# Two changes of written order in a decoder layer: sums ahead of low parts in gate and up, and one step of putting together per pair in down

## The chip, the cores and the metric

The kernel runs on one core of one Trainium2 chip. The number that counts is the device time of one execution in microseconds (us). The kernel before was timed three times: 2296.75 us is the median, 2289.06 the lowest and 2296.81 the highest. A further execution was recorded by the profiler; every duration below comes from it.

The engines of the core are named as in the profile: PE (TensorE, matrix products; PEld is its loading of weights), DVE (VectorE, elementwise on two inputs), ACT (ScalarE, elementwise on one input), POOL (GpSimd, here an issuer of transfers and a little elementwise work) and SP (SyncE, here the issuer of most transfers). Each engine takes its own instructions strictly in its own order; between engines there are only semaphores.

## The reference

One layer of a decoder on 512 tokens of width 2048, in fp32: an RMS norm, attention with two groups of heads, an output projection and a residual add; then a second RMS norm and a SwiGLU block with 5632 hidden columns, and a residual add. The change touches the last part alone:

```
def _swiglu(h, w_gate, w_up, w_down):
    return (jax.nn.silu(h @ w_gate) * (h @ w_up)) @ w_down
...
        h = _rms_norm(x, ffn_norm[l])
        x = x + _swiglu(h, w_gate[l], w_up[l], w_down[l])
```

## The kernel before

**Numbers in two parts.** PE multiplies in a rounded fp32 type. To keep fp32 accuracy each operand is split: ACT copies it into the rounded type, which gives the high part (`act(..., AF.Copy)`), and DVE subtracts that copy from the operand, which gives the low part (`tt(..., op=OP.subtract)`). Three products (high by high, high by low, low by high) then stand for one.

**Seven products in place of eight.** Gate, up and down use a scheme in which a product of 2 by 2 blocks takes seven block products of sums and differences of blocks in place of eight. The sums of the weight blocks are made on the chip; the results are put together again afterwards.

**Gate and up** (the loop from line 866 on) work on 176 groups of weights: 22 pairs of hidden column blocks `j`, gate and up of each (`which`), and four groups `g` along the contraction. Group `i` has these steps:

- `fetch(i)` (line 701): SP loads a 512 KB tile `r` of four weight blocks. There are three such buffers, so `fetch(i + 4)` can be issued only when everything that reads group `i + 1`'s tile is done. The last of these is the low part.
- `sums(i)` (line 713): three DVE additions that write four more blocks into the same tile.
- `parts(i)` (line 728, by `part_steps`): ACT writes the high part of seven blocks (1792 columns), DVE the low part. They go into one of two halves of `bigm`, so group `i` writes where group `i - 2` was. The copy on ACT also paces one transfer from the POOL queue per group (`sum_weights`, line 112), which adds up weight blocks of down in device memory for later.
- 42 matmuls (line 901): 28 with the high part of the weights, then 14 with the low part.
- `next(pending)` (line 920): one step of the work behind an earlier column block. `evict` reads the finished sums from PSUM, `gate_out` multiplies by the norm's factor and applies SiLU, `up_out` multiplies gate by up, forms block sums and stores them as `ad` for down. Four steps after a gate block and four after an up block fill the eight groups of a pair `j`.

The order of all this on each engine is the order in which the program writes it, because `pin` (line 67) tells the scheduler to keep it from the last output projection on. Matmuls are placed by the scheduler. In group `i` the kernel before writes: `parts(i + 1)`, `fetch(i + 4)`, `sums(i + 2)` (lines 877 to 881), the matmuls, `next(pending)`.

**Down** runs four passes over 22 pairs of hidden blocks (`ps_` = 0 to 3; two halves of the output, each with a first pass of four products and a second of three). For each pair `splits` (line 836) makes high and low parts of a down weight tile and of an activation tile, and PE runs 48 matmuls in the first passes, 36 in the second. PSUM holds the sums of one pass. `keep1` saves those of a first pass in `ca` and `cb`; `finish_late` (line 956) puts the results of the first half of the output together, block by block (`q` = 0 to 3), in steps that are taken during the third pass (`ps_` = 2). Two steps are taken per pair of that pass, one in the others (lines 1022 and 1023). A step is a DVE addition, subtraction or product; two of them also need the residual, which POOL loads into the single buffer `acc` from `x1d`, and POOL stores the result to `out`. `fold` and `fold_early` do the same for the second half of the output in the last pass, and `finish` ends the kernel.

Of the kernel before, what the change touches and what calls it, by code (L numbers as in the profile page):

```python
# [62 lines left out]
def hybrid_layer(ctx: ExitStack, tc: tile.TileContext, xT, vec, ffb, wfg, wfirst, win, cmpw, wout, wgu, wdn, out):  # L63
# [772 lines left out]
    def splits(i):  # L836
        second, j = pass_of(i)[1:]
        n = 3 if second else 4
        m, at = WAT[i % 4]
        w = [cut(m, at + h * 4 * T, n * T) for h in range(2)]  # L840
        m, at = AAT[i % 3]
        a = [cut(m, at + h * 4 * 256, n * 256) for h in range(2)]
        split2(a, rawa.pop(i))
        if second:
            r, t = raww.pop(i), t2(j)
            tt(r[:, T:2 * T], r[:, :T], t, op=OP.add)
            split2([x[:, 2 * T:] for x in w], t)
            split2([x[:, :2 * T] for x in w], r[:, :2 * T])
        else:
            split2(w, raww[i])  # L850
        return [[x.rearrange("p (f c) -> p f c", f=n) for x in y] for y in (w, a)]

    SETS = (("s", "s", "t", "o"), ("g", "g", "m", "t"))
# [16 lines left out]
    for j in range(NJ):  # L870
        for which in range(2):
            q = [ps.tile([P, T], F32, tag=tag, name=f"q{which}{j}_{i}", bufs=BUFS[tag])
                 for i, tag in enumerate(SETS[which])]
            for g in range(NG):
                i = (2 * j + which) * NG + g

                if 3 <= i < LAST:
                    parts(i + 1)
                    fetch(i + 4)
                if 2 <= i < LAST - 1:  # L880
                    sums(i + 2)
                if i == 4:
                    split(fr2, acc)
                if i == LAST - 2:
                    live["fa"] = ffp.tile([P, 2 * FORM + OFF_FORM], F32, tag="fa", name="rawm", bufs=1)
                    for n in range(2):
                        load_a(n)
                        run(load_w(n))
                elif i >= LAST - 1:
                    ahead[i - LAST + 1] = splits(i - LAST + 1)  # L890
                w = split_w.pop(i)

                for wp in range(2):
                    for kk in range(2):
                        k = 2 * (ORDER[i] % NG) + kk
                        a = forms[k]
                        cs = slice(kk * P, (kk + 1) * P)
                        for fa, fb, b, h in PROD:
                            o = q[b][:, h * 256:(h + 1) * 256]
                            for xp in range(2 - wp):  # L900
                                nc.tensor.matmul(o, w[:, wp, fb, cs], a[:, xp, fa],  # L901
                                                 start=(k == 0 and h == 0 and wp == 0 and xp == 0),
                                                 stop=(g == NG - 1 and kk == 1 and wp == 1), skip_group_check=True)
# [33 lines left out]
    def fold(y, s4, s62=None):  # L937

        tt(halves(y[1]), halves(y[1]), both(s4), op=OP.subtract)
        yield  # L940
        tt(y[0][:, :256], y[0][:, :256], y[1][:, :256], op=OP.subtract)
        yield
        if s62 is not None:
            tt(y[0], y[0], s62, op=OP.add)
            yield

    def fold_early(q):

        y = [k[:, q] for k in kept]
        yield from fold(y, y[0][:, 256:])  # L950
# [5 lines left out]
    def finish_late(q, b):  # L956
# [3 lines left out]
        act(s4, b[1][:, :256], AF.Copy)  # L960
        yield
        y = [k[:, q] for k in kept]
        tt(s4, s4, y[0][:, 256:], op=OP.add)
        yield from fold(y, s4, s62)
        for i in range(2):
            pin(nc.gpsimd.dma_start(acc, x1d[2 * q + i]))
            tt(y[i], y[i], rstd, op=OP.mult)
            yield
            tt(y[i], y[i], acc, op=OP.add)
            pin(nc.gpsimd.dma_start(out[2 * q + i], y[i]))  # L970
            yield

    def finish(q, b):

# [12 lines left out]
    for ps_ in range(4):  # L987
# [16 lines left out]
        def block(js, parts, end=None):  # L1004
# [124 lines left out]
```

## Time and profile before

| | us |
|---|---|
| median of three runs (lowest, highest) | 2296.75 (2289.06, 2296.81) |
| the profiled execution | 2287.78 |
| its span, first to last instruction | 2286.0 |
| PE busy | 2187.9 |
| DVE busy | 1703.7 |
| ACT busy | 1007.0 |

In the span, the groups of gate and up run from 875 us to 1842 us, down from there to the end. Times in a row of the profile count from the span's start. In the view of groups of instructions, a row gives the line, the engine, the operation, the tile that is written and those read, shapes and count; then the busy time in us and the mean of one instruction in ns; then the engine's idle time just before these instructions, and who ended it. Line 71 is `tt` and line 74 `act`, the helpers that record every such operation, so that the tile's name tells which one it is: `bigm<-r,bigm` on DVE is a low part, `bigm<-r` on ACT a high part, `r<-r` on DVE the sums, and `q` the matmuls of gate and up; `pd` are those of down. Matmuls overlap in PE's pipeline: a row that says 280 ns for one of them does not mean that each takes 280 ns of PE's time.

### The profile page before, as it was taken

The page shows a single profiled execution, that of the slowest core. Times are in us where ns is not written, and L with a number is a line of the kernel's source. Part 1 is how long each engine was busy: PE and PEld are TensorE (multiplying, and loading weights), DVE is VectorE, ACT ScalarE, POOL GpSimd, SP SyncE. Part 2 cuts the span into 40 slices and gives each one's busy share as a digit, 9 for nine tenths or more (in the row PEclk, how much of TensorE's full clock was granted, in tenths as well). Part 3 has the DMA queues.
Part 4 walks back from the last instruction along what each step waited for, and adds up shares of the span by engine and source line. Part 5 has one row for each costly group of instructions (what it writes and reads, how often), then busy time and mean ns, then how long its engine had stood idle before and what let it go on. Part 6 is the DMA issues. An engine that isn't in the chain of part 4 may idle for free.

```text
span 2286.0 us, 37104 instructions
## 1 busy us (share of the span) xinstructions
PE 2187.9 (96%) x15207; PEld 1984.8 (87%) x15207; DVE 1703.7 (75%) x2488; ACT 1007.0 (44%) x1231; POOL 172.6 (8%) x283
## 2 busy tenths in 40 slices
PE   8999999999999999999999999999999999999898
PEld 6878878788787889888888888898888899999898
DVE  5677577555565547888878888888888897888888
ACT  5555455444454334333333333333333355564453
POOL 0000000000100000111111111111111100000000
PEclk9999999999999999999999999999999999999999
DMA  5421211222223444667766666766666698468854
GB/s 180 148 65 38 74 47 56 75 81 76 77 80 106 142 153 136 160 161 172 163 163 166 165 165 158 177 162 163 172 161 162 164 356 299 147 230 286 292 155 144
DMA packets 111740, 347.47 MB, mean 152 GB/s; under 512 B 13392, under 2 KB 13392, under 8 KB 111568
## 3 DMA queue, kind: packets, MB, share of 16 engines
q1 hardware_dynamic: 83808, 268.21, 35.5%
q0 software_dynamic: 22144, 52.44, 14.0%
q10 hardware_dynamic: 5616, 24.43, 3.3%
q8 instruction: 119, 1.95, 0.3%
q14 instruction: 53, 0.43, 0.1%
HBM read 316.46 MB, written 74.71 MB: 171 GB/s over the span
## 4 chain that ended last, share of the span: by engine, by line
PE 50%; DVE 28%; ACT 14%; issue 6%; DMA 2%; POOL 0%; ACTq 0%; SPq 0%; DVEq 0%; POOLq 0%
DVE bigm L71 14%; ACT bigm L74 12%; DVE r L71 9%; PE pd L1029 7%; PE q L901 5%; PE pd L1034 4%; PE po L143 2%; PE po L141 2%; PE po L142 2%; DVE cb L71 2%; DMA acc<-x1d 1%; PE ps_qf L141 1%; PE ps_qf L142 1%; PE ps_qf L143 1%; PE ps_vf L141 1%
## 5 line engine op out<-in xcount | busy, mean ns | idle before, releaser
L74 ACT ACTIVATE bigm<-r 128x1792 fp32r<-128x1792 f32 x175 | 298.4, 1705 | 604.7 <-DVE r L71 478.1
L71 DVE TENSOR_TENSOR bigm<-r,bigm 128x1792 fp32r<-128x1792 f32 x175 | 354.3, 2024 | 149.0 <-ACT bigm L74 149.0
L71 DVE TENSOR_TENSOR r<-r 128x512 f32<-128x512 f32 x525 | 268.7, 512 | 14.6 <-DMA r<-wgu 2.5
L901 PE MATMUL q<-formy,bigm 128*128 128x256 f32 x1848 | 223.8, 280 | 20.5 <-ACT bigm L74 20.5
L901 PE MATMUL q<-forma,bigm 128*128 128x256 f32 x1848 | 224.7, 281 | 17.6 <-ACT bigm L74 17.6
L901 PEld LDWEIGHTS q<-formy,bigm 128*128 128x128 f32 x1848 | 215.3, 188 | 28.9 <-ACT bigm L74 28.9
L901 PE MATMUL q<-bigm 128*128 128x256 f32 x1848 | 224.3, 280 | 16.1 <-ACT bigm L74 16.1
L901 PE MATMUL q<-formx,bigm 128*128 128x256 f32 x1848 | 223.8, 280 | 16.2 <-ACT bigm L74 16.2
L901 PEld LDWEIGHTS q<-forma,bigm 128*128 128x128 f32 x1848 | 216.2, 189 | 26.2 <-ACT bigm L74 26.1
L901 PEld LDWEIGHTS q<-bigm 128*128 128x128 f32 x1848 | 215.8, 188 | 24.4 <-ACT bigm L74 24.4
L901 PEld LDWEIGHTS q<-formx,bigm 128*128 128x128 f32 x1848 | 215.2, 188 | 24.5 <-ACT bigm L74 24.5
L116 POOL DMA_DIRECT2D wsum<-wdn x176 | 120.1, 682 | 1016.9 <-ACT bigm L74 901.7
L1029 PE MATMUL pd<-bigm 128*128 128x256 f32 x1224 | 153.0, 280 | 8.8 <-DVE bigm L71 6.2
L1029 PEld LDWEIGHTS pd<-bigm 128*128 128x128 f32 x1224 | 146.6, 191 | 10.2 <-DVE bigm L71 6.8
L71 DVE TENSOR_TENSOR bigm<-wd,bigm 128x2048 fp32r<-128x2048 f32 (+1 forms) x64 | 110.3, 1724 | 26.6 <-ACT bigm L74 26.6
L74 ACT ACTIVATE bigm<-wd 128x2048 fp32r<-128x2048 f32 (+1 forms) x64 | 93.7, 1465 | 72.6 <-DVE wd L71 50.8
L143 PE MATMUL po<-bigm,wp_o 128*128 128x512 f32 x256 | 99.8, 390 | 0.8 <-DVE wp_o L71 0.8
L141 PE MATMUL po<-bigm,wp_o 128*128 128x512 f32 x256 | 99.8, 390 | 0.0
L142 PE MATMUL po<-bigm,wp_o 128*128 128x512 f32 x256 | 99.6, 389 | 0.0
L74 ACT ACTIVATE bigm<-rawm 128x768 fp32r<-128x768 f32 (+2 forms) x72 | 65.7, 921 | 62.4 <-PE pd L1034 57.7
L71 DVE TENSOR_TENSOR bigm<-rawm,bigm 128x768 fp32r<-128x768 f32 (+2 forms) x72 | 75.9, 1054 | 12.1 <-ACT bigm L74 12.0
L1034 PE MATMUL pd<-bigm 128*128 128x256 f32 x612 | 81.3, 277 | 0.0
(478 smaller groups left out, 4092.3 us busy)
## 6 DMA issues: line engine op xcount, KB each, us to landing
r<-wgu SPq DMA_DIRECT2D x175, 512.0 KB, 4.5
wsum<-wdn POOLq DMA_DIRECT2D x176, 256.0 KB, 4.8
rawm<-ad SPq DMA_DIRECT2D x44, 512.0 KB, 6.3
wd<-wdn SPq DMA_DIRECT2D x40, 512.0 KB, 5.8
wd<-wsum SPq DMA_DIRECT2D x40, 512.0 KB, 6.7
ad<-cb ACTq DMA_DIRECT2D x22, 896.0 KB, 4.6
rawm<-ad SPq DMA_DIRECT2D x44, 384.0 KB, 3.7
ws_o<-wout SPq DMA_DIRECT2D x32, 512.0 KB, 3.5
```

The lines of the kernel that those rows point to most:

```text
L71: return pin(nc.vector.tensor_tensor(*args, op=op))
L74: return pin(nc.scalar.activation(*args, **kw))
L116: d = nc.gpsimd.dma_start(step[0], step[1], **step[2])
L141: nc.tensor.matmul(o, lh, rh, start=start, stop=False)
L142: nc.tensor.matmul(o, lh, rl, start=False, stop=False)
L143: nc.tensor.matmul(o, ll, rh, start=False, stop=stop)
L901: nc.tensor.matmul(o, w[:, wp, fb, cs], a[:, xp, fa], start=(k == 0 and h == 0 and wp == 0 and xp == 0), stop=(g == NG - 1 and kk == 1 and ...
L1029: nc.tensor.matmul(b[q][k][:, h * 256:(h + 1) * 256], w[0][:, fb, q * P:(q + 1) * P], a[xp][:, fa], start=(j == 0 and h == 0 and xp == 0), ...
L1034: nc.tensor.matmul(b[q][k][:, h * 256:(h + 1) * 256], w[1][:, fb, q * P:(q + 1) * P], a[0][:, fa], start=False, stop=(j == NJ - 1), skip_g ...
```

## The change

In the loop of gate and up `sums(i + 2)` is written ahead of `parts(i + 1)` and `fetch(i + 4)`. `finish_late` is written anew: five steps per block `q` in place of seven, one step per pair in the third pass in place of two, block 1 ahead of block 0, and each load of the residual is issued two steps ahead of the step that adds it. `fold` goes into `fold_early` without a change to what that does. In the very last of the 88 pairs of down, the activation tile is split after the weight tile.

```
@@ splits
-        split2(a, rawa.pop(i))
+        if i < 4 * NJ - 1:
+            split2(a, rawa.pop(i))
...
         else:
             split2(w, raww[i])
+        if i == 4 * NJ - 1:
+            split2(a, rawa.pop(i))
@@ gate and up, group i
+                if 2 <= i < LAST - 1:
+                    sums(i + 2)
                 if 3 <= i < LAST:
                     parts(i + 1)
                     fetch(i + 4)
-                if 2 <= i < LAST - 1:
-                    sums(i + 2)
@@ finish_late
         y = [k[:, q] for k in kept]
-        tt(s4, s4, y[0][:, 256:], op=OP.add)
-        yield from fold(y, s4, s62)
-        for i in range(2):
+
+        def residual(i):
             pin(nc.gpsimd.dma_start(acc, x1d[2 * q + i]))
-            tt(y[i], y[i], rstd, op=OP.mult)
-            yield
+
+        def put(i):
             tt(y[i], y[i], acc, op=OP.add)
             pin(nc.gpsimd.dma_start(out[2 * q + i], y[i]))
-            yield
+
+        residual(1)
+        tt(s4, s4, y[0][:, 256:], op=OP.add)
+        tt(halves(y[1]), halves(y[1]), both(s4), op=OP.subtract)
+        yield
+        tt(y[0][:, :256], y[0][:, :256], y[1][:, :256], op=OP.subtract)
+        tt(y[0], y[0], s62, op=OP.add)
+        yield
+        tt(y[1], y[1], rstd, op=OP.mult)
+        put(1)
+        residual(0)
+        yield
+        tt(y[0], y[0], rstd, op=OP.mult)
+        yield
+        put(0)
+        yield
@@ block
-            for _ in range(1 + (ps_ == 2)):
-                next(pending, None)
+            next(pending, None)
```

More of the change, by code (lines that the diff above doesn't have):

```diff
@@ L935, in keep1, with fold_early @@
         tt(halves(kept[1][:, q]), halves(b[1]), both(kept[0][:, q, :256]), op=OP.add)
-    def fold(y, s4, s62=None):
-        tt(halves(y[1]), halves(y[1]), both(s4), op=OP.subtract)
+    def fold_early(q):
+        y = [k[:, q] for k in kept]
+        tt(halves(y[1]), halves(y[1]), both(y[0][:, 256:]), op=OP.subtract)
         yield
@@ L942, in fold @@
         yield
-        if s62 is not None:
-            tt(y[0], y[0], s62, op=OP.add)
-            yield
-    def fold_early(q):
-        y = [k[:, q] for k in kept]
-        yield from fold(y, y[0][:, 256:])
         for i in range(2):
@@ L962, in finish_late @@
         y = [k[:, q] for k in kept]
-        tt(s4, s4, y[0][:, 256:], op=OP.add)
-        yield from fold(y, s4, s62)
-        for i in range(2):
+        def residual(i):
             pin(nc.gpsimd.dma_start(acc, x1d[2 * q + i]))
-            tt(y[i], y[i], rstd, op=OP.mult)
-            yield
+        def put(i):
             tt(y[i], y[i], acc, op=OP.add)
             pin(nc.gpsimd.dma_start(out[2 * q + i], y[i]))
-            yield
+        residual(1)
[13 more added lines that the diff above has]
+        yield
     def finish(q, b):
```

## The prediction

> **What bounds the kernel now.** I read the page's engine shares first, then the groups of instructions, the list of waits, the chain that ended last, and then one stretch of gate and up in order of time.
>
> ```profile
> span 2286.0 us, 37104 instructions
> PE 2187.9 (96%) x15207; PEld 1984.8 (87%) x15207; DVE 1703.7 (75%) x2488; ACT 1007.0 (44%) x1231; POOL 172.6 (8%) x283
> L74 ACT ACTIVATE bigm<-r 128x1792 fp32r<-128x1792 f32 x175 | 298.4, 1705 | 604.7 <-DVE r L71 478.1
> L71 DVE TENSOR_TENSOR bigm<-r,bigm 128x1792 fp32r<-128x1792 f32 x175 | 354.3, 2024 | 149.0 <-ACT bigm L74 149.0
> L71 DVE TENSOR_TENSOR r<-r 128x512 f32<-128x512 f32 x525 | 268.7, 512 | 14.6 <-DMA r<-wgu 2.5
> PE q L901 <- ACT bigm L74: 70.4, 169, 2.0
> ```
>
> PE looks full at 96%, but in 169 of 176 groups it waits for a high part, the high parts wait for the sums (478.1 us), and the low parts wait for the high parts (149.0 us). That is a ring of two engines that wait for each other in turn. In order of time (start, duration, engine):
>
> ```profile
> 1304.18 2.02 DVE L71 TENSOR_TENSOR bigm<-r,bigm 128x1792 fp32r<-128x1792 f32 x1 [0.84 <-ACT bigm L74]
> 1304.20 5.05 PE L901 MATMUL q<-formy,bigm 128*128 128x256 f32 x42 [0.67 <-ACT bigm L74]
> 1306.13 1.60 DVE L71 TENSOR_TENSOR r<-r 128x512 f32<-128x512 f32 x3
> 1307.90 1.71 ACT L74 ACTIVATE bigm<-r 128x1792 fp32r<-128x1792 f32 x1 [3.75 <-DVE r L71]
> 1309.64 2.02 DVE L71 TENSOR_TENSOR bigm<-r,bigm 128x1792 fp32r<-128x1792 f32 x1 [0.98 <-ACT bigm L74]
> 1309.66 5.04 PE L901 MATMUL q<-bigm 128*128 128x256 f32 x42 [0.41 <-ACT bigm L74]
> ```
>
> Low part of one group, sums of the next, its high part, its low part: 1304.18 to 1306.13 (1.95), to 1307.90 (1.77), to 1309.64 (1.74), together 5.46 us. This is the distance of the two matmul groups as well (1304.20 to 1309.66). So a ring of DVE and ACT, and no engine by itself, sets the period. Over the stage:
>
> ```profile
> 897.46 6.66 PE L901 MATMUL q<-forma,bigm 128*128 128x256 f32 x42 [2.03 <-ACT bigm L74]
> 1836.89 5.04 PE L901 MATMUL q<-formy,bigm 128*128 128x256 f32 x42 [0.41 <-ACT bigm L74]
> 900.00:1820.00 920.00, 853.40 (x7047) 820.69 (x7045) 759.49 (x1010) 323.47 (x239) 113.54 (x167) 1.00 0.67 164
> ```
>
> The first two rows are the starts of group 4 and of group 175: 939.43 us for 171 groups, 5.494 each. In the third (length, then busy time of PE, PEld, DVE, ACT, POOL) DVE is busy 759.49 of 920 us, which is 4.54 us per group of 5.494.
>
> **The change part by part. Gate and up.** Nothing is added or removed; the three sums move ahead of the low part, and with them past the low part's wait. The high part of group i + 2 needs the sums of i + 2, and these no longer stand behind the low part of i + 1. The ring falls apart: DVE makes the sums while ACT makes the high part. On SP the fetch still follows the low part, so it moves later by no more than DVE does. POOL's one transfer per group follows the high part as before. What bounds the period then?
>
> PE. Its pitch without waits shows where groups touch:
>
> ```profile
> 885.37 5.11 PE L901 MATMUL q<-formy,bigm 128*128 128x256 f32 x42
> 890.32 5.11 PE L901 MATMUL q<-bigm 128*128 128x256 f32 x42
> 1865.72 3.63 PE pd L1029 x32
> 1871.16 3.63 PE pd L1029 x32
> ```
>
> The upper pair are two touching groups: 4.95 us for 42 matmuls, 117.8 ns each. The lower pair, from the chain, are two touching pairs of down: 5.44 us for 48 matmuls, 113.3 ns each, or 4.76 us for 42. PE has two paces, and I cannot say which one it will keep. The 5.05 us of a group's row hide this, as the last matmul's drain is in it.
>
> The Trainium skill ("TensorE: Matmul & The Clock Gate", Back-to-back issue gap) gives 256/2.4 + 2.5 = 109 ns for a warm matmul of 256 columns. By that a group would take 4.59 us, and DVE's load would be the bound at about the same value; both paces in the rows are slower, and I go by the rows.
>
> DVE. 4.54 us of work per group, and the steps behind a column block are uneven; the heaviest is this one:
>
> ```profile
> 1340.37 0.68 DVE L71 TENSOR_TENSOR cb<-ca 128x512 f32<-128x512 f32 x1
> 1341.09 1.61 DVE L71 TENSOR_TENSOR cb<-cb 128x512 f32<-128x512 f32 x3
> ```
>
> With it a group costs 1.95 + 1.54 + 2.27 = 5.8 us on DVE, above PE's 4.76 to 4.95, but the lightest has 3.5. A low part is needed only after 28 matmuls (3.2 us) of its own group and may be written as soon as the group two before is done, so about 4 us of lateness cost PE nothing. DVE at 92 to 95% fits.
>
> The Trainium skill ("GPSIMD Engine Reference", Key points) says that GpSimd shares its SBUF interfaces with DVE and contends with DVE instructions of two SBUF inputs, which all of these are. That speaks against a plan that leaves DVE hardly any idle time. The row that bears on it, with its POOL partner:
>
> ```profile
> L71 DVE TENSOR_TENSOR bigm<-r,bigm x146: 2015/2026/2027, 1002.2 to 1798.4; 128x1792 fp32r<-128x1792 f32 x146
> L116 POOL DMA_DIRECT2D wsum<-wdn x176: 523/782/867, 874.3 to 1837.1; - x176
> ```
>
> POOL issues beside nearly every one of these low parts, and they spread by 12 ns (shortest, median, longest). DVE is not lengthened; if it were by POOL's whole 0.78 us, its load would be 5.32 us.
>
> The load of weights. The sums of group n now stand ahead of the low part of n - 1, so a late tile stops that too. A new ring appears: low part of n - 3, fetch of n into its buffer, sums of n, low part of n - 1, over two groups.
>
> ```profile
> r<-wgu SPq DMA_DIRECT2D x175, 512.0 KB, 4.5
> DMA to landing us min/median/max: 3.3/4.5/7.9
> ```
>
> At the median it is 4.5 + 1.60 + 2.02 = 8.1 us per two groups, 4.1 each, so the load is hidden. If each took the longest 7.9, it would be 5.8 each, worse than now. Single slow ones are taken up by the lateness that PE allows; today DVE waited 2.5 us for them in all.
>
> PE without any wait would be 4.76 to 4.95; I put 0.05 on the middle for tiles that land late and take 4.90 us. The bounds are 4.76 and, for slower landings at the higher rate (the engines of DMA are already busy at 0.67), 5.30. Saved: 171 x (5.494 - 4.90) = 101.6 us; 125.5 and 33 at the bounds.
>
> **The handover to down.** The first loads of down go into a buffer that PE frees three groups before the end, and PE waits for them:
>
> ```profile
> 1828.25 0.45 SPq L792 DMA_DIRECT2D rawm<-wsum  x1
> 1843.04 1.91 ACT L74 ACTIVATE bigm<-rawm 128x2048 fp32r<-128x2048 f32 x1 [1.95 <-DMA rawm<-wsum]
> 1845.01 2.10 PE L1029 MATMUL pd<-bigm 128*128 128x256 f32 x16 [1.26 <-ACT bigm L74]
> ```
>
> The load does not get shorter, so the 3 x 0.6 us that the last three groups gain come back as wait here: 1.8 us lost (0 to 3).
>
> **Down, third pass.** These are the places where PE stops, and what DVE waited for:
>
> ```profile
> DVE ca L71 <- DMA acc<-x1d: 16.8, 4, 5.6
> acc<-x1d POOLq DMA_DIRECT2D x8, 256.0 KB, 7.2
> 2092.95 3.80 PE L1029 MATMUL pd<-formx,bigm 128*128 128x256 f32 x31 [1.32 <-DVE formx L71]
> 2117.15 0.69 DVE L71 TENSOR_TENSOR ca<-ca,acc 128x512 f32<-128x512 f32 x1 [5.58 <-DMA acc<-x1d]
> 2120.09 5.40 PE L1029 MATMUL pd<-bigm 128*128 128x256 f32 x31 [4.45 <-DVE bigm L71]
> 2139.57 3.78 PE L1029 MATMUL pd<-bigm 128*128 128x256 f32 x31 [1.28 <-DVE bigm L71]
> ```
>
> PE loses 1.32 + 4.45 + 1.28 = 7.05 us, each time after DVE stood in front of `acc`, plus 1.6 us as the 31 matmuls at 2120.09 take 5.40 in place of 3.8: 8.65. After the change a residual is issued two pairs (10.9 us) ahead of its use, against 7.2 to land, so those waits go. DVE's load:
>
> ```profile
> 2082.56 1.22 DVE L71 TENSOR_TENSOR bigm<-rawm,bigm 128x1024 fp32r<-128x1024 f32 x1
> 2083.69 2.28 DVE L71 TENSOR_TENSOR bigm<-wd,bigm 128x2048 fp32r<-128x2048 f32 x1
> 2085.90 0.68 DVE L71 TENSOR_TENSOR t2m<-wd 128x512 f32<-128x512 f32 x1
> ```
>
> 4.18 us per pair, and a block's putting together is six operations of 0.69 and two of 0.42, 4.98 us. At seven steps, two per pair, that was 1.42 per pair: 5.60 of 5.44, overfull even without waits. At five steps, one per pair, it is 1.0: 5.18 of 5.44. Twenty steps fit the 21 pairs ahead of the last block. The fullest step (a product and an addition) makes 5.56, and the next is lighter. I take 8 us saved; the bounds are 0 (DVE too full after all) and 9.
>
> **The last pair** changes which copy ACT makes first. PE's stops there:
>
> ```profile
> 2265.13 0.85 PE L1029 MATMUL pd<-bigm 128*128 128x256 f32 x5 [1.31 <-ACT bigm L74]
> 2267.84 1.06 ACT L74 ACTIVATE bigm<-wd 128x1024 fp32r<-128x1024 f32 x1 [1.51 <-DVE wd L71]
> ```
>
> ACT idles 1.51 us before the last weight copy, into which nothing new moves; DVE makes the activation's low part (0.95) last instead. Between 1.3 saved and 2 lost; I take 0, as it is one place with both signs.
>
> **Sum.** 101.6 - 1.8 + 8 = 107.8. The profiled execution (2287.78) would become 2180.0. The three runs lay 1.3 to 9.0 us above it, so I add the middle, 5: 2185 us.
>
> **The rivals.**
> - PE keeps the faster pace of 113.3 ns without a stop: 125.5 - 2.1 + 8 saved, 2161. For it: down holds that pace for a hundred us; against: DVE at 95% and the slowest tiles must then never show.
> - The load of weights becomes the bound: a median of 6.5 us in place of 4.5 makes the new ring (6.5 + 3.62)/2 = 5.06, and with jitter up to 5.30; 2211 to 2254. For it: the same bytes in less time, and tiles of 7.9; against: the median leaves 1.4 us per two groups or more.
> - Slower: the same ring from a mean landing of 7.4 us on, where (7.4 + 3.62)/2 exceeds 5.494. At 8 us it would be 5.81 and 171 x 0.32 = 54 us lost, 2340. Only the slowest of 175 loads is there now.
> - The order does not do what it says, since a high part or low part waits for PE's halves of `bigm` where I see none: the period stays near 5.4, 2285. Against it: the rows show DVE in written order, and the low parts' idle time is put down to ACT alone.
> - DVE is stretched by POOL to 5.32 us per group: 30 + 6 saved, 2257; the spread of 12 ns speaks against.
> - A pitch of 109 ns, with DVE as the bound at 4.6: 153 + 6 saved, 2134. No row has it.
>
> **How the numbers follow.** Forecast, 4.80 to 5.00 per group, 2168 to 2202: 0.58. Faster pace 0.17, load of weights 0.14, no effect 0.04, slower 0.03, POOL 0.02, 109 ns 0.02. 2185 is the forecast's. The range 2155 to 2235 leaves out the last four and some 0.04 of the load's case. About 0.5% (11 us) is what a measurement of this kernel can tell from no change: faster 0.94, same 0.03, slower 0.03.
>
> **What would show it.** Right: the wait of high parts for sums shrinks from 478 us to under 100, PE's for high parts from 70 to under 15, groups 4.8 to 5.0 apart, DVE above 90% in the stage. Wrong: DVE idle before `r<-r`, released by the load (now 2.5 us); matmul groups that still wait for `bigm`; a fetch that lands after 6 us at the median. In the third pass `ca` no longer waits for `acc`, and PE has no stop over 1 us; the start of down shows a longer wait for `rawm`.

## The result, and the profile after

| us | before | after |
|---|---|---|
| median of four executions (lowest, highest) | 2292.9 (2288.9, 2296.81) | 2164.1 (2157.06, 2199.43) |
| the profiled execution | 2287.78 | 2157.06 |
| its span | 2286.0 | 2155.4 |
| on another chip, eleven executions before and six after: median (lowest, highest) | 2292.73 (2286.51, 2297.04) | 2186.65 (2154.51, 2201.4) |

The ratio after to before is 0.943, with a 95% interval of 0.938 to 0.948, in the first comparison and 0.952 (0.949 to 0.955) in the second. These ratios leave out executions more than 1.5% above the fastest of the same kernel, so the plain median of all ten executions of the changed kernel, 2178.6, says more. Why its executions lie so far apart is a subject of the experiments below.

The page of the changed kernel, the lines that answer to those of before (engine shares, the chain's shares by engine, groups):

```profile
span 2155.4 us, 37105 instructions
PE 2129.1 (99%) x15207; PEld 1959.9 (91%) x15207; DVE 1698.9 (79%) x2488; ACT 1006.9 (47%) x1231; POOL 172.1 (8%) x283
...
PE 89%; DVE 4%; ACT 3%; issue 2%; DMA 1%; POOL 0%; SPq 0%; ACTq 0%; DVEq 0%; POOLq 0%
...
L74 ACT ACTIVATE bigm<-r 128x1792 fp32r<-128x1792 f32 x175 | 299.9, 1714 | 477.0 <-PE q L904 287.8
L71 DVE TENSOR_TENSOR bigm<-r,bigm 128x1792 fp32r<-128x1792 f32 x175 | 353.6, 2021 | 13.3 <-ACT bigm L74 12.4
L71 DVE TENSOR_TENSOR r<-r 128x512 f32<-128x512 f32 x525 | 268.7, 512 | 28.4 <-DMA r<-wgu 16.2
L904 PE MATMUL q<-forma,bigm 128*128 128x256 f32 x1848 | 218.6, 277 | 2.3 <-ACT bigm L74 2.3
...
r<-wgu SPq DMA_DIRECT2D x175, 512.0 KB, 4.3
```

And from its list of waits (total us, times, longest):

```profile
ACT bigm L74 <- DVE r L71: 28.9, 14, 5.6
```

The busy times of DVE and ACT are what they were. What changed is who waits for whom. The high parts hardly wait for the sums any more (28.9 us, 478.1 before) but for PE to free their half of `bigm` (287.8); the low parts' wait for high parts shrank from 149.0 to 12.4 us; PE's wait for high parts from 70.4 to 2.3. The chain that ended last now runs through PE for 89% of the span.

In order of time, in the same part of gate and up as before (start, duration, engine):

```profile
1304.40 4.92 PE L904 MATMUL q<-formx,bigm 128*128 128x256 f32 x42
1304.81 2.03 DVE L71 TENSOR_TENSOR bigm<-r,bigm 128x1792 fp32r<-128x1792 f32 x1 [0.17 <-ACT bigm L74]
1307.68 1.60 DVE L71 TENSOR_TENSOR r<-r 128x512 f32<-128x512 f32 x3
1307.82 1.72 ACT L74 ACTIVATE bigm<-r 128x1792 fp32r<-128x1792 f32 x1 [3.04 <-DVE ca L71]
1309.16 4.92 PE L904 MATMUL q<-formy,bigm 128*128 128x256 f32 x42
1309.57 2.03 DVE L71 TENSOR_TENSOR bigm<-r,bigm 128x1792 fp32r<-128x1792 f32 x1 [0.28 <-ACT bigm L74]
```

The sums (1307.68) and the high part (1307.82) now run side by side: they belong to different groups. No matmul row has a bracket, so PE waits for nothing, and two groups are 1309.16 - 1304.40 = 4.76 us apart. Over one stretch of the stage (length, busy time of PE, PEld, DVE, ACT, POOL, each with its count; granted clock of PE; share of DMA; GB/s):

```profile
900.00:1700.00 800.00, 800.00 (x7055) 799.93 (x7054) 758.60 (x1017) 325.82 (x241) 114.39 (x168) 1.00 0.74 190
```

DVE is busy 758.60 of 800 us, 95%. By stage, from the starts of the first matmuls of each:

| stage | before | after | difference | forecast |
|---|---|---|---|---|
| gate and up, start of group 4 to start of group 175 | 939.43 | 816.5 | -123.0 | -101.6 |
| first pass of down, with the waits of the handover in it | 121.70 | 123.85 | +2.15 | +1.8 |
| second pass of down | 89.80 | 89.79 | 0.0 | 0 |
| third pass | 129.81 | 119.68 | -10.1 | -8 |
| fourth pass | 96.47 | 95.64 | -0.8 | 0 |
| from the start of the last matmul | 6.44 | 7.88 | +1.4 | 0 |

With 0.2 us ahead of group 4, 0.1 in group 175 and 0.1 outside the span that is the 130.7 us between the two profiled executions.

### The profile page after: what moved, and what is told of

It reads as the page before. It is cut to its first block, busy times and chain, and to the rows that moved or that the text cites. A ratio compares the mean times of both kernels' runs of the same rounds, so it can differ in the third digit from the quotient of the medians.

```text
span 2155.4 us, 37105 instructions
## 1 busy us (share of the span) xinstructions
PE 2129.1 (99%) x15207; PEld 1959.9 (91%) x15207; DVE 1698.9 (79%) x2488; ACT 1006.9 (47%) x1231; POOL 172.1 (8%) x283
## 3 DMA queue, kind: packets, MB, share of 16 engines
q8 instruction: 119, 1.95, 0.4%
## 4 chain that ended last, share of the span: by engine, by line
PE 89%; DVE 4%; ACT 3%; issue 2%; DMA 1%; POOL 0%; SPq 0%; ACTq 0%; DVEq 0%; POOLq 0%
PE q L904 37%; PE pd L1038 10%; PE pd L1043 5%; PE po L143 2%; PE po L141 2%; PE po L142 2%; PE ps_qf L141 1%; PE ps_qf L142 1%; PE ps_qf L143 1%; PE ps_vf L141 1%; PE ps_vf L143 1%; PE ps_vf L142 1%; DVE bigm L71 1%; PE ps_kf L141 1%; PE ps_qn L141 1%
## 5 line engine op out<-in xcount | busy, mean ns | idle before, releaser
L74 ACT ACTIVATE bigm<-r 128x1792 fp32r<-128x1792 f32 x175 | 299.9, 1714 | 477.0 <-PE q L904 287.8
L71 DVE TENSOR_TENSOR bigm<-r,bigm 128x1792 fp32r<-128x1792 f32 x175 | 353.6, 2021 | 13.3 <-ACT bigm L74 12.4
L71 DVE TENSOR_TENSOR r<-r 128x512 f32<-128x512 f32 x525 | 268.7, 512 | 28.4 <-DMA r<-wgu 16.2
L904 PE MATMUL q<-forma,bigm 128*128 128x256 f32 x1848 | 218.6, 277 | 2.3 <-ACT bigm L74 2.3
L904 PE MATMUL q<-formy,bigm 128*128 128x256 f32 x1848 | 217.0, 276 | 0.0
L904 PE MATMUL q<-formx,bigm 128*128 128x256 f32 x1848 | 216.8, 276 | 0.0
L904 PE MATMUL q<-bigm 128*128 128x256 f32 x1848 | 216.7, 276 | 0.0
```

The lines of the kernel that those rows point to most:

```text
L71: return pin(nc.vector.tensor_tensor(*args, op=op))
L74: return pin(nc.scalar.activation(*args, **kw))
L904: nc.tensor.matmul(o, w[:, wp, fb, cs], a[:, xp, fa], start=(k == 0 and h == 0 and wp == 0 and xp == 0), stop=(g == NG - 1 and kk == 1 and ...
```

## The experiments

### The exchange in gate and up alone

```
@@ kernel before, gate and up, group i
+                if 2 <= i < LAST - 1:
+                    sums(i + 2)
                 if 3 <= i < LAST:
                     parts(i + 1)
                     fetch(i + 4)
-                if 2 <= i < LAST - 1:
-                    sums(i + 2)
```

> The kernel before with the sums written ahead of the low part in gate and up, and nothing else. If the ring of DVE and ACT was the whole of it: groups 4.76 us apart without a stop of PE as in the changed kernel (or 4.95 apart, if PE keeps its slower pace), 123 us less in gate and up, 2 us more at the handover; together 2167 us in an execution like the profiled one, 2200 with the slower pace. If down's part was needed for it (for instance since less work in down frees transfers): well above 2200 in every run, and groups that still wait for their high parts. The third pass of down stays at 129.8 us by the first, since nothing of it is changed.

Measured: 2198.66 (profiled), 2166.08, 2204.4, 2197.05, against a median of 2290.16; the ratio is 0.952 (0.944 to 0.960). The waits of this kernel (waiting engine, tile and line, whom it waits for; total us, times, longest), its matmul groups in order of time, and a stretch of its stage:

```profile
ACT bigm L74 <- PE q L901: 429.2, 141, 3.2
```

```profile
1303.99 5.11 PE L901 MATMUL q<-formy,bigm 128*128 128x256 f32 x42
1308.94 5.11 PE L901 MATMUL q<-bigm 128*128 128x256 f32 x42
```

```profile
920.00:1720.00 800.00, 800.00 (x6795) 800.00 (x6794) 733.24 (x977) 308.10 (x224) 110.00 (x162) 1.00 0.75 184
```

The ring is gone and PE never stops here either, but its groups are 4.95 us apart (846.25 us for 171) and not 4.76. DVE has slack in this execution (733.24 of 800), and PE is the one that others wait for, so the 0.19 us per group are PE's own. The granted clock is 1.00 in this stretch and in that of the changed kernel alike. So the exchange alone takes the ring away, and what remains is a PE with two paces: 117.8 ns per matmul here, 113.3 in the changed kernel's profile. The slower pace set in inside group 8: groups 7, 8 and 9 start at 913.46, 918.22 and 923.10 us, 4.76 and then 4.88 apart, and from there on it is 4.95. Within group 8 two matmuls start 175 ns apart instead of 113, and behind that point the pace is 118. The times fit the two values that were expected, 2167 and 2200. The third pass of down, which this edit does not touch, took 132.09 us against 129.81, so two executions of the same pass can differ by 2 us. The two paces were the open point from here on.

### The new `finish_late` alone

The diff is that of the change for `finish_late`, `fold_early` and `block`, on the kernel before.

> The kernel before with the new putting together alone (five steps, one per pair, residual issued two steps ahead). If the residual's wait and the overfull DVE caused the third pass's stops: that pass goes from 129.8 us to 119.7 (22 pairs at 5.44), DVE no longer waits for acc, and the kernel is 10 us faster, 2278 in an execution like the profiled one. If another stop comes in its place (DVE at 5.18 of 5.44 per pair): 125 us or more for the pass. Gate and up stays at 5.49 us per group.

Measured: median 2279.1 over ten executions against 2290.16, ratio 0.9955 (0.9936 to 0.9974). Gate and up stayed at 5.494 us per group. The third pass took 119.68 us without a stop of PE, as in the changed kernel. One stretch of that pass, first of the kernel before, then of this one:

```profile
2060.00:2170.00 110.00, 102.96 (x884) 102.36 (x883) 90.35 (x85) 55.01 (x37) 8.09 (x15) 0.98 0.84 292
```

```profile
2060.00:2170.00 110.00, 110.00 (x973) 110.00 (x972) 100.88 (x95) 59.16 (x43) 8.07 (x15) 1.00 0.88 310
```

884 matmuls in 110 us became 973: PE is full. This part of the change is worth its 10 us without the other one.

### The last pair's order alone

```
@@ kernel before, splits
-        split2(a, rawa.pop(i))
+        if i < 4 * NJ - 1:
+            split2(a, rawa.pop(i))
...
+        if i == 4 * NJ - 1:
+            split2(a, rawa.pop(i))
```

> The kernel before with the other order of the last pair's splits alone. The fourth pass of down took 96.47 us before and 95.64 in the changed kernel. If that difference is this edit: 95.6 here, with two stops of PE in its last 20 us in place of five. If it is chance, or comes from the third pass: 96.4 again. Either way under 1.5 us of the whole, which a total of one execution cannot show; the pass in the trace can.

Measured: 2297.8 in a single execution; its first two passes of down ran at PE's slower pace, so only the fourth pass and the end are read. PE's last stops, of this kernel and of the kernel before (one of 0.49 us stands ahead of them in both):

```profile
2274.64 2.15 PE L1032 MATMUL pd<-bigm 128*128 128x256 f32 x16 [1.31 <-ACT bigm L74]
2278.37 0.74 PE L1032 MATMUL pd<-formx,bigm 128*128 128x256 f32 x4 [1.58 <-ACT formx L74]
```

```profile
2265.13 0.85 PE L1029 MATMUL pd<-bigm 128*128 128x256 f32 x5 [1.31 <-ACT bigm L74]
2266.38 0.39 PE L1029 MATMUL pd<-formx,bigm 128*128 128x256 f32 x1 [0.40 <-ACT bigm L74]
2267.26 0.58 PE L1029 MATMUL pd<-formx,bigm 128*128 128x256 f32 x1 [0.25 <-DVE formx L71]
```

PE now stops once for 1.58 us where it stopped twice, for 0.40 and 0.25, and takes the matmuls in larger runs. The fourth pass is 95.66 in place of 96.47, but the work behind the last matmul is 7.87 in place of 6.44: 0.8 won, 1.4 lost. Both numbers are those of the changed kernel (95.64 and 7.88). How the time divides between pass and end varies without this edit too (94.72 and 7.47 in the exchange alone), so their sum is the better measure: 102.9 us in the kernel before, 103.0 with the new `finish_late` alone and 102.2 with the exchange alone, against 103.5 here and in the changed kernel's two profiles. This part of the change costs 0.6 us or a little more.

### One step per pair, with the old seven steps

Changed kernel, but with the old `fold` and the old body of `finish_late` (each residual issued one step ahead of its use).

> The changed kernel with the old seven steps of putting together, one per pair: the residual is issued one step ahead of its use, and 28 steps do not fit the 21 pairs ahead of the last block, so seven are left to be taken at once before it. If the waits for the residual were the cause: one pair (5.44 us) is less than the 7.2 us that it takes to land, so DVE still waits some 2 us eight times, but these waits are partly in DVE's spare time; the pass comes out at 121 to 126 us, with its stop at the end, where the seven steps (4.98 us of work and up to two waits of 7 us) stand ahead of the last block. If the number of steps per pair was the cause and not the residual: 119.7 us up to the last block.

Measured: 2197.12 in a single execution, with gate and up at the slower pace (4.956 per group), so again only the pass is read. The third pass took 125.72 us. DVE waited for `acc` once for 3.6 and once for 1.8 us, where four waits took 16.8 us in the kernel before. ACT's and PE's longest stops at the end of that pass:

```profile
2081.05 1.09 PE L1031 MATMUL pd<-bigm 128*128 128x256 f32 x7 [1.54 <-DVE bigm L71]
2083.25 1.23 PE L1036 MATMUL pd<-bigm 128*128 128x256 f32 x4 [1.11 <-DVE bigm L71]
2085.30 1.06 ACT L74 ACTIVATE bigm<-wd 128x1024 fp32r<-128x1024 f32 x1 [10.06 <-DVE wd L71]
```

With one step per pair PE ran through the pass without a stop up to 2081 us even with the old body. The stops at its end have the cause that was expected: 28 steps do not fit, the seven of the last block were taken at once, and both waits for `acc` fall among them.

That DVE would wait some 2 us for each residual was expected too, and did not happen. An issue two steps ahead was there already, since POOL issues the load right behind the addition that frees `acc`, a step ahead of where it is written:

```profile
1981.80 0.68 DVE L71 TENSOR_TENSOR cb<-cb,acc 128x512 f32<-128x512 f32 x1
1983.33 0.54 POOL L969 DMA_DIRECT2D acc<-x1d  x1
1992.67 0.68 DVE L71 TENSOR_TENSOR ca<-ca,acc 128x512 f32<-128x512 f32 x1
```

The issue follows 1.5 us after the start of the addition that frees the buffer, here and in the kernel before (2062.07 and 2063.61). At one step per pair the next addition then comes 9.3 us after the issue, and the load lands in 7.7; in the kernel before the load landed in 6.92 us, and DVE had by then waited 3.33 us with its next addition.

### The new five steps, two per pair

```
@@ changed kernel, block
-            next(pending, None)
+            for _ in range(1 + (ps_ == 2)):
+                next(pending, None)
```

> The changed kernel with its new five steps taken two per pair in the third pass, so that the residual is issued one pair ahead of its use and all is done after ten pairs. If the early residual was what mattered: the third pass stays within 1 us of 119.7. If spreading DVE's work was: DVE has 4.18 + 2.0 = 6.2 us of work in each of ten pairs of 5.44, 7 us too much, and the residual (7.2 us to land) comes late again; stops of PE of several us in the first ten pairs, and a pass of 124 to 130 us. I expect the second.

Measured: 2195.64 in a single execution, gate and up at the slower pace (4.958). The third pass took 128.29 us, close to the 129.81 of the kernel before, with five stops. One of them in order of time:

```profile
2008.31 0.69 DVE L71 TENSOR_TENSOR cb<-cb,acc 128x512 f32<-128x512 f32 x1 [2.29 <-DMA acc<-x1d]
2011.25 3.81 PE L1039 MATMUL pd<-bigm,formx 128*128 128x256 f32 x31 [2.25 <-DVE bigm L71]
```

The residual is still issued two steps ahead, but two steps are now one pair (5.44 us), less than the 5.7 us in which it lands here at the median (7.2 in the kernel before), and DVE stands in front of it again. DVE also has more work per pair, as the expectation says; this run does not separate the two. Together the two runs say that one step per pair removed the stops inside the pass; the new body, which fits all its steps into the pass, is needed for the end of it.

### How much room DVE has

```
@@ changed kernel, sums: the last sum is made twice (and, in a second kernel, three times)
+        tt(r[:, 7], r[:, 6], r[:, 3], op=OP.add)
```

> The changed kernel with the last of the three sums of each group made twice (0.43 us more of DVE, the same result). DVE had 4.52 us of work per group of 4.76. If DVE is the next bound: 4.52 + 0.43 + small gaps = 4.95 to 5.1 us per group, 33 to 58 us more than 2157, and PE stops again before the groups. If DVE has more room than its busy time says (its waits for the high parts are only PE's halves of bigm not being free): under 4.85 per group, and under 2175.

> The same with the last sum made three times (0.85 us more of DVE). If DVE is the bound then: 4.52 + 0.85 = 5.4 to 5.5 us per group, that is 0.43 more than with two, so the slope is one. That is the period of the kernel before, so about 2265 to 2285 us. If the old ring (low part, sums, high part) still held in any form, it would be 5.46 + 0.85 = 6.3.

Measured: 2207.95 with 5.034 us per group, and 2286.03 with 5.483. The stretch 930 to 1730 of the first:

```profile
930.00:1730.00 800.00, 783.15 (x6705) 774.20 (x6704) 779.04 (x1118) 307.52 (x220) 108.57 (x160) 1.00 0.64 181
```

DVE is busy 779.04 of 800 and now the bound; ACT's high parts stand behind the sums again (404.8 us in the whole kernel). From one to two extra additions the period grew by 0.449 us, about an addition's 0.43 with the start of one, so by this straight line (an estimate) DVE's own limit without an extra one is 5.034 - 0.449 = 4.585 us per group. Against 4.76 that leaves 0.18 us, 4% of a group. The change fits, but hardly.

### How much room the load has

```
@@ changed kernel, fetch: 256 KB more per weight tile, into columns that the sums overwrite
+        load(r[:, 4:6].rearrange("p f c -> p (f c)"), wgu[i // NG % 2, i // NG // 2, ORDER[i] % NG][:, :T])
```

> The changed kernel with 256 KB more loaded into each weight tile ahead of its 512 KB (blocks 4 and 5, which the sums then overwrite). If the load of weights has the room that the ring of load, sums and low part leaves (landing up to 2 x 4.76 - 3.62 = 5.9 us; 4.3 at the median now): landing rises to 5 to 6 us and the period to 4.76 to 4.9. If the load is already nearly the bound: 5.1 us per group or more, with DVE idle before the sums, released by the load. I expect the upper end of the first: 4.8 to 4.9, since single slow loads now pass 6 us more often.

Measured: 2229.69 and 5.153 us per group, outside what was expected. DVE's groups from 930 to 1750, and the two loads on the page:

```profile
L71 DVE TENSOR_TENSOR r<-r 128x256 f32<-128x256 f32 (+1 forms) x477 | 244.7, 513 | 98.3 <-DMA r<-wgu 86.9
```

```profile
r<-wgu SPq DMA_DIRECT2D x175, 512.0 KB, 5.5
r<-wgu SPq DMA_DIRECT2D x175, 256.0 KB, 3.2
```

From the end of a low part to the last landing it took 6.0 us in the mean, against 4.5 in the changed kernel. The expectation reckoned with a mean landing in the ring of two groups, which gives (6.0 + 3.62)/2 = 4.81 here, and so saw hardly a cost. But DVE takes its work in order and has only some 0.18 us per group to make up for what a tile is late. It idled 98.3 us in front of the 159 groups' sums, 0.62 each, and 98.3 us over 159 groups with the 4.52 us of its work (758.60 over 168 groups in the changed kernel) is 5.14. The load's limit is thus met earlier than by the ring's mean.

### The changed kernel again

Six more executions (profile included), to see how the times lie.

> The changed kernel once more. If PE keeps one of two paces for the whole of gate and up, drawn once at its last stop ahead of the stage: the times fall into two clumps, about 2157 (4.76 us per group) and about 2190 (4.95 per group, 171 x 0.19 = 32 us more), with few between. If the spread of 2157 to 2199 is something else (transfers, the clock): the times lie evenly between, and groups stand at other distances than 4.76 or 4.95.

Measured: 2154.51 (profiled), 2168.46, 2188.34, 2186.78, 2186.53, 2201.4. The first four executions had 2157.06, 2157.56, 2170.64 and 2199.43. Two clumps were expected; the times stand in four, near 2156, 2169, 2187 and 2200. The profiled one ran at 4.766 us per group. The slower pace in gate and up alone would add 169 x 0.19 = 32 us, in the passes of down some 14 (0.16 us for a pair of 36 matmuls, 0.22 for one of 48, 88 pairs, less where it lasts for some passes only): 2155, 2169, 2187, 2201. That each execution of a clump ran at the pace of that clump is this arithmetic; only the profiled ones were seen.

### A stop every sixteen groups

One more matmul at the start of every 16th group, which reads the high part of the next group just as it is written, and so makes PE stop. Its result is overwritten.

```
@@ changed kernel, the products of a group
+                            if wp == kk == 0 and n == 1 and i % 16 == 0 and i:
+                                nc.tensor.matmul(q[3][:, :256], split_w[i + 1][:, 0, 0, :P], a[:, 0, 0],
+                                                 start=True, stop=False, skip_group_check=True)
```

> The changed kernel with one matmul more in every sixteenth group of gate and up (ten in all; its result is overwritten), which reads the high part that ACT is just then writing for the next group, and so stops PE for some tenths of a us. If each stop draws the pace anew, with one chance in four for the slower one as after the stops of the kernel before: the slower pace shows in some 25% of the groups in every execution, all times lie close together at 2157 + 8 + 10 x 0.4 = 2169, between the two clumps of the changed kernel. If the pace does not hang on stops: the clumps stay, each 2 to 4 us higher.

Measured: 2174.04 to 2183.26 in five executions and 2167.15 in one; median 2176.53, on the chip of the six above. PE's rows at the first of these stops:

```profile
951.88 5.11 PE L907 MATMUL q<-bigm 128*128 128x256 f32 x42
...
958.12 0.38 PE L903 MATMUL q<-forma,bigm 128*128 128x256 f32 x1 [0.90 <-ACT bigm L74]
...
962.88 4.92 PE L907 MATMUL q<-formx,bigm 128*128 128x256 f32 x42
```

A group's row of 5.11 us belongs to the slower pace, 4.92 to the faster. In the profiled execution (2183.21) the pace was slow from group 9 to 15, fast 16 to 31, slow 32 to 47, fast 48 to 63, slow 64 to 79, fast 80 to 127, slow 128 to 143 and fast to the end. From group 9 on it changed at these stops and nowhere else. After a stop on the slower pace the faster one followed four times of four, on the faster one the slower three times of six: a stop draws anew, and between stops the pace stays. The slower pace held in 55 of these 167 groups, a third where a quarter was expected, and the other nine stops were shorter than the one shown (0.12 to 0.2 us by the distance of the starts). No run has an extra matmul of 256 columns without a stop, so what the matmul itself does is not told apart here from the stop.

### Short matmuls without a stop

One more matmul at the start of every 8th group that waits for nothing, of 252, 250, 128 and 254 columns in turn, its result overwritten.

```
@@ changed kernel, the products of a group
+                            if wp == kk == 0 and n == 1 and i % 8 == 0 and i:
+                                m = (254, 252, 250, 128)[i // 8 % 4]
+                                nc.tensor.matmul(q[3][:, :m], w[:, 0, 0, :P], a[:, 0, 0, :m],
+                                                 start=True, stop=False, skip_group_check=True)
```

> The changed kernel with one matmul more in every eighth group of gate and up (21 in all, result overwritten) that waits for nothing, of 252, 250, 128 and 254 columns in turn in place of 256. If a stop of PE is needed to draw the pace anew: one pace through all 21, times in the clumps of the changed kernel plus 21 x 0.1 = 2 us. If the pace is only how loads and matmuls fall against each other, an odd length shifts that too: the pace changes at some of the 21, most of all at the 128, and the times lie between the clumps, near 2170.

Measured: 2194.93, 2194.87, 2195.99, 2196.6. The changed kernel's spread of 47 us is down to 1.7. All four lie above the 2170 that was expected. PE's rows at groups 24, 40 and 64 (128, 252 and 254 columns):

```profile
993.70 5.11 PE L908 MATMUL q<-bigm 128*128 128x256 f32 x42
...
998.88 0.22 PE L904 MATMUL q<-forma,bigm 128*128 128x128 f32 x1
...
1003.55 4.92 PE L908 MATMUL q<-formx,bigm 128*128 128x256 f32 x42
...
1070.31 4.92 PE L908 MATMUL q<-bigm 128*128 128x256 f32 x42
...
1075.30 0.27 PE L904 MATMUL q<-forma,bigm 128*128 128x252 f32 x1
...
1080.12 5.11 PE L908 MATMUL q<-formx,bigm 128*128 128x256 f32 x42
...
1189.18 5.11 PE L908 MATMUL q<-bigm 128*128 128x256 f32 x42
...
1194.36 0.28 PE L904 MATMUL q<-forma,bigm 128*128 128x254 f32 x1
...
1199.02 4.92 PE L908 MATMUL q<-formx,bigm 128*128 128x256 f32 x42
```

No row has a bracket, so no stop is needed: the width of one matmul settles the pace of hundreds that follow. 252 columns turned the faster pace into the slower one five times of five and once left the slower one, 254 turned the slower into the faster four times of four and once left the faster one; 250 left the slower one as it was; 128 turned it once (here) and else left it. So the slower pace held for nearly three quarters of the stage, and in the profiled execution through the first three passes of down as well, which is why the times are high.

### The changed kernel with nine such matmuls

254 columns at groups 8, 24, 64, 112 and 160, and one near the start of each pass of down.

```
@@ changed kernel, the products of a group
+                            if wp == kk == 0 and n == 1 and i in (8, 24, 64, 112, 160):
+                                nc.tensor.matmul(q[3][:, :254], w[:, 0, 0, :P], a[:, 0, 0, :254],
+                                                 start=True, stop=False, skip_group_check=True)
@@ block
+                if js[0] == 0 and 3 in qs:
+                    j, w, a = ws[0]
+                    nc.tensor.matmul(b[3][0][:, :254], w[0][:, 0, :P], a[0][:, 0, :254],
+                                     start=True, stop=False, skip_group_check=True)
```

> The changed kernel with nine more matmuls of 254 columns (results overwritten): in five groups of gate and up (8, 24, 64, 112, 160) and one near the start of each pass of down. In the run before, a matmul of 254 columns brought the faster pace each time that the slower one ran (four times) and kept it the one time that the faster one ran. If that holds in general: every execution runs gate and up at 4.76 us per group and passes 1 and 2 of down at 89.8 and 119.7 us, all times lie within a few us of 2157, and none is near 2169, 2187 or 2200. If those five cases were chance: the clumps of the changed kernel come back.

Measured: 2159.11 (profiled), 2160.82, 2159.14, 2159.36, 2165.14; median 2159.36, ratio to before 0.9431 (0.9409 to 0.9453). The changed kernel's ten executions spread over 47 us around 2178.6; these five over 6. In the profiled one the faster pace was there before group 8, so gate and up show only that it is kept. The first pass of down, however, began at the slower pace, and there the rows show the turn:

```profile
1727.92 0.28 PE L1050 MATMUL pd<-formx 128*128 128x256 f32 x1
...
1729.81 0.28 PE L1039 MATMUL pd<-formx 128*128 128x254 f32 x1
...
1731.75 1.98 PE L1045 MATMUL pd<-bigm 128*128 128x256 f32 x16
1733.56 0.28 PE L1050 MATMUL pd<-formx 128*128 128x256 f32 x1
```

Sixteen matmuls take 1.89 us ahead of the one of 254 columns (1727.92 to 1729.81, 118 ns each) and 1.81 us behind it (1731.75 to 1733.56, 113 each). That the slower pace was cured in the other four executions is read from their times alone, and why one of them took 2165.14 was not seen. This kernel beats the kernel before in every execution, and the changed one in the median and in its spread; the changed kernel's best executions (2154.51 to 2157.56) are a few us faster than it.

## Why the prediction was right, and where a step was not

**Gate and up.** The diagnosis held: a ring of DVE and ACT set 5.494 us, the written order made it, and with the exchange alone PE became the bound. Most of the prediction's signs came as named: the high parts' wait for sums fell to 28.9 us (under 100 was said), PE's wait for them to 2.3 (under 15), and DVE is above 90% busy. The groups' distance did not: 4.76 us in the profile, just below the 4.8 to 5.0 that was named.

**The mis-sized term is "take 4.90 us".** It was the middle of two paces seen in the rows plus 0.05 for late tiles. The middle does not exist: in a stage without stops PE holds one pace to the end, 4.76 us per group in the profiled execution and 4.95 in that of the exchange alone, so the gain is 123 or 93 us and not 101.6. The allowance for late tiles was not needed: the load's median landing went from 4.5 to 4.3 us, and though DVE waited 16.2 us in all for tiles (2.5 before), PE did not stop for it. The profiled execution, 2157.06, is therefore the rival called "PE keeps the faster pace" (2161, given 0.17), while five of the ten executions lie between 2168 and 2189, nearer to the forecast of 2185, and two near 2200. That the median of the ten, 2178.6, lies close to the forecast is luck in this respect: it is the middle of clumps, and no execution lies between 2171 and 2186. A better text would have named two cases, 2161 and about 2190, and asked what draws between them.

**The Trainium skill's pitch** ("TensorE: Matmul & The Clock Gate", Back-to-back issue gap) of 256/2.4 + 2.5 = 109 ns, which the page gives for a single matmul by itself, was not reached in any run's stream: 113.3 and 117.8 are what the rows show, with 1.00 as the granted clock.

**DVE's load** fits, as said, but the margin the prediction gave by the lateness that PE allows (about 4 us once) is no margin in the mean. The margin in the mean is 0.18 us per group, by the two runs with extra sums.

**POOL** did not stretch DVE's low parts: 2021 ns in the mean after, 2024 before, with the same 176 transfers issued beside them in a shorter stage. The contention that the Trainium skill names ("GPSIMD Engine Reference", Key points) is not seen in these rows, even with DVE at 95%. POOL only issues transfers in this stage, so the rows say nothing of elementwise work on POOL.

**The load of weights.** It stayed hidden, as taken. But the formula of that rival, (landing + 3.62)/2, was wrong: with more bytes per tile the period rose to 5.15 us where the formula gave 4.81, since the lateness that PE allows takes up a late tile, as the prediction put it, only while DVE has time to catch up. The bound of 5.30 and the slower case at a landing of 7.4 us thus lay nearer than the prediction said; how near isn't measured beyond this one size. The rival of no effect has a slip as well: 5.4 us per group and 8 us in the third pass give about 2269, not 2285.

**The handover.** Between the two profiled executions the first pass grew by 2.15 us, 1.8 forecast. The rows (changed kernel):

```profile
1713.76 4.92 PE L904 MATMUL q<-formy,bigm 128*128 128x256 f32 x42
1718.52 1.98 PE L1038 MATMUL pd<-formx 128*128 128x256 f32 x16
1720.80 1.91 ACT L74 ACTIVATE bigm<-rawm 128x2048 fp32r<-128x2048 f32 x1 [4.41 <-DMA rawm<-wsum]
1722.76 3.36 PE L1038 MATMUL pd<-bigm 128*128 128x256 f32 x16 [2.27 <-ACT bigm L74]
```

ACT waits 4.41 us for that load (1.95 before), PE 2.27 for ACT (1.26 before). But this does not show the forecast cause. With the old order in gate and up, the run of the new `finish_late` alone has a wait of PE of 3.36 us here and a first pass of 124.99; with the new order, the changed kernel's second profile has 122.68 and the exchange alone 123.69. The load itself took 13.0 to 17.0 us from issue to landing in these traces. One execution differs from another by more than the 1.8 us, so the agreement is luck, and whether the handover costs anything is open.

**The third pass** gave 10.1 us for a forecast of 8 and an upper bound of 9. The bound was PE's idle time plus the 1.6 us that one series of 31 matmuls took longer; part of what lies above it is that the pass also ran at the slower pace for a while in the kernel before, since each of its stops drew anew (about 0.6 us by the matmuls' distances); the rest was not traced. The mechanism was half named. The prediction put it on a residual issued two pairs, 10.9 us, ahead of its use, and on DVE's load; the runs with one half each show that the step per pair does most of it, as it doubles the time between one use of `acc` and the next. The 10.9 us are not reached, because the issue waits for the buffer: in the changed kernel the first block's second load is issued at 1942.79, lands in 6.59 us and is used at 1950.04, 7.25 us after its issue. So this stage has little room as well.

**The last pair** was taken as 0 between -1.3 and +2, and is +0.6 or a little more, a gain inside the pass and a larger loss behind the last matmul that the prediction had not looked at.

## What to carry to other kernels

Where two engines each wait for the other in turn and neither is full, look for the one operation in the written order that the next round needs and that stands behind a wait it does not need itself; moving it adds no work, but look for the new ring that it makes (here that of the loads). When the ring is gone, ask how much the next engine has to spare per round (an extra operation of known length on it measures this in one run), because lateness in an engine that takes its work in order is made up only from its spare time. And where a kernel's times stand in clumps, look at the distance of touching matmul groups in the trace before averaging them.

## What the runs showed of the hardware

PE has two paces for the same work at the same granted clock: 113.3 and 117.8 ns per matmul of 256 columns with its weight load, 4% apart. The pace is drawn when PE starts again, and kept while it does not stop: over the last 167 of 176 groups in the changed kernel's profile. A stop can be very short, as the two starts 175 ns apart in group 8 of the exchange alone show. In three kernels with the old order in gate and up (the kernel before, the new `finish_late` alone, the last pair alone) 507 groups start after a stop, and 106 of them, 21%, then run at the slower pace: 20% of those that follow the faster pace, 23% of those that follow the slower one. It goes with the length of the stop: counted over these three and the kernels with two extra sums and with the larger load, at 690 ns from the last matmul's start to the next one's, 16 of 19 starts gave the slower pace, at 688, 689, 691 and 692 ns none of 82. These lengths were picked out of the counts afterwards. Without a stop, one matmul of 252 columns set the slower pace five times of five and one of 254 the faster five times of five. All this would fit two streams of PE (weight loads and matmuls) that can stand in one of two positions to each other; no run shows such positions, so the mechanism stays open. The paces can also make up much of the 8 us by which the kernel before spread: its passes of down take the one or the other, as 93.28 us for the second pass with the last pair's order alone shows, against 89.80.

A stop also costs more than its idle time in the rows. Between the touching groups of 4.76 us and those of the kernel before at the faster pace (1304.20 to 1309.66, 5.46) lie 0.70 us, and the bracket of the second says 0.41. Of the rest, 0.16 us is the end of the last matmul, which counts as busy (its row lasts 0.28 us where the next start would come after 0.113 without a stop), and 0.12 is a slower start: a group behind a stop lasts 5.04 us, one without a stop 4.92.
